# A hybrid decoder layer on one core: all projections first, attention, inverses and recurrence one or more stages behind

## The chip, the cores and the metric

One core of a Trainium2 chip runs one program; the time is device microseconds of one execution. The engines are TensorE (PE, matmuls, with its weight loads as PEld), VectorE (DVE), ScalarE (ACT), GpSimd (POOL) and SyncE (SP, which here issues nearly all DMAs). Each runs its own instructions in order and waits on semaphores for the others.

## The reference

Cut to what is computed: 2,048 new positions and 8 sequences of 8 decoded ones go through one layer of width 1024.

```
h = rmsnorm(x, norm_attn);  p = h @ w_in                  # 512 q, 128 k, 128 v, 1792 rwkv, 2048 gates
o_attn = sliding-window attention (window 128, sinks), 8 q heads on 2 kv heads
o_rwkv = RWKV-7 on the 1792: token shift, lora decay w and rate a, then per position
         S = S * w + (S a) b^T + v k^T ;  y = S r           # 8 heads, S is 64 x 64
         group norm, bonus, gate
merged = sigmoid(g0) * (o_attn @ w_branch_attn) + sigmoid(g1) * (o_rwkv @ w_branch_rwkv)
x = x + merged @ w_out
u = rmsnorm(x, norm_ffn) @ w_ffn_in                        # 2 x 2816
x = x + (gelu(causal conv of width 3 over u0) * u1) @ w_ffn_out
y = rmsnorm(x, norm_final)                                 # and the new caches and states
```

## The kernel before

**Tiling.** The 2,112 columns (positions, then decoded tokens) are cut into three blocks of 704, and a block into halves of 384 and 320. Values lie transposed, features on partitions. Weights and activations are float32, each split into a high part and a rest (`split`, `unit`), and a product is three matmuls: high by high, high by rest, rest by high (`mm3`). A unit is one load of 128 x 1024 weights; ACT casts its high part (L335), and POOL or, for every third unit, DVE computes the rest (L341). A unit meets one block in 48 matmuls, 24 for each half. These dense matmuls write the tile `psd` (three PSUM banks); everything else on PE uses `psr` (three banks) and `psc` (two).

**Stages of a block.** `inputs`: 36 units of `w_in`, of which 14 feed the recurrence (`proj_rwkv`, with `prep` and `keynorm` making per-chunk operands, written to DRAM), 6 attention, and 16 the gates. Then `attn_prompt` (pieces of 128 positions by two groups of heads), `inverse` (per half, triangular inverses of 64 x 64 by elimination on DVE), `recur` (`chain`: 11 chunks of 64 positions, each with three handovers from PE to DVE or ACT and back, then `groupnorm`), `gather` (loads the branch outputs and splits them into the operand `os`), `merge` (8 units of `w_br` and 8 of `w_out`), and `ffn` (66 units).

**What sets the order.** The code emits dense work in sequence. Background work consists of generators in queues (`push`); before each k-step `mm3` calls `tick`, and `step` advances a generator by one piece when a model of the engines' clocks says that its operands will be there (`account`, `open`). `drain` advances queues without any dense work until they are empty. A scheduler then fixes each engine's order. Before, `inputs(0)` runs with the load of the next `h` beside it; `rest(0)` (attention and inverses together, then the recurrence) is queued behind it and runs beside `inputs(1)`. Four gate units of block 1 are held back; `early_merge` queues the gather of block 0, runs them, drains, and merges. The FFN of block 0 has `rest(1)` and `next_h(2)` beside it; then `inputs(2)`, the merge of block 1, its FFN with `rest(2)` and the gather of block 2, and the merge and FFN of block 2.

**Names in the steps.** `h` is the split, normed input of a block (two buffers in turn); `normed` (L431, L345, L346) makes one of its eight columns. `cvu`, `cm`, `car`, `ckb`, `cq` are the operands of a chunk, loaded one chunk ahead (L1103 and around), `cx` the solution's copy (L1121), `S` the state (L1164, L1165). `ol` are the branch outputs in `gather` (L1277), two buffers; `gt` the gate tiles (two). LAG (L30) puts the last tiles of `w_out` in the order (6,0), (7,0), (6,1), (7,1). In an inverse L1057 and L1063 are transposes of 32 x 32 blocks.

Of the kernel before, what the change touches and what calls it, by code (L numbers as in the profile page):

```python
# [17 lines left out]
P = 128  # L18
# [30 lines left out]
for _name, _w in (("ident", 128), ("maskp", 128), ("sel", 2), ("selm", 2), ("ones", 1), ("cj", 128),  # L49
                  ("blk", 128), ("bm", 8), ("m65", 390), ("att", 256), ("masks", 128), ("m65s", 332)):  # L50
    CST[_name] = (_n, _w)
    _n += _w
# [50 lines left out]
class Kernel:  # L103
    def __init__(self, tc, i, o, es):
# [8 lines left out]
        self.kp_ = pool("keep", 2)  # L113
# [5 lines left out]
        self.anchor, self.inside = {}, False  # L119
# [40 lines left out]
    def setup(self):  # L160
# [3 lines left out]
        for name in ("cj", "blk"):  # L164
            self.cr[name] = cp.tile([P, CST[name][1]], F32R, name=f"{name}r")
            nc.gpsimd.tensor_copy(self.cr[name], self.cst(name))
# [71 lines left out]

    def account(self):
# [4 lines left out]
        for k in range(self.seen, m):  # L244
# [5 lines left out]
            if engine in ("DVE", "Activation"):  # L250
                if self.inside:
                    if engine in self.anchor:
                        self.tc.add_manual_dep(ins, self.anchor[engine], mybir.DependencyInfo(
                            mybir.DependencyClass.NoSync, mybir.DependencyReason.DATA), reason="after the dense work before it")
                elif any(hasattr(a, "bass_ap") and a.bass_ap.tensor.name.startswith("psd") for a in ins.ins):
                    self.anchor[engine] = ins.name
            if engine == "PE":
                t["PE"] += c
# [16 lines left out]
    def tick(self):  # L275

        self.account()
        for q in self.streams.values():
            self.step(q)
# [5 lines left out]
    def step(self, q):  # L285
        t = self.clock
        if not q or q[0][1] > t["PE"] or self.open() > t["PE"]:
            return
        self.account()
        entry = q[0]  # L290
        self.inside = True
# [14 lines left out]
        entry[1] = max(entry[1], at + entry[3])  # L306

# [143 lines left out]
    def start(self, hp, xp):  # L451
# [4 lines left out]
        self.ct = self.cp.tile([P, CST["m65"][0]], F32, name="ct")  # L456
# [12 lines left out]
        nc.sync.dma_start(self.ct, self.i["cst"][:, :CST["m65"][0]])  # L469
# [41 lines left out]
    def load_h(self, b, hp):  # L511

        h = self.bigtile(hp, "h")
        self.push("n", self.load_steps(b, h))
        return h
# [97 lines left out]
    def attn_prompt(self, b, ap):  # L613
        nc = self.nc
        npr = T if b < 2 else T - TS
# [51 lines left out]
        items = [(t0, g) for t0 in range(0, npr, 128) for g in range(2)]  # L667
        fs = {0: front(0)}
        yield 4.0
        fs[0] = halves(fs[0])  # L670
        fr = front(128)
        yield 0.2
        sm = {0: (yield from head(fs[0], 0))}
# [295 lines left out]
    def mtile(self, b, pp, name):  # L969


        if b == 1 and name == "kt":
            return self.tp.tile([P, 2, 384], F32, tag="xv", name="kt", bufs=2)[:].rearrange("p a c -> p (a c)")[:, :512].rearrange("p (c j) -> p c j", j=128)
        return pp.tile([P, 4, 128], F32, tag="m", name=name, bufs=2 if b == 1 else 4)

    def headsum(self, sq, sel, least, eps, k):

        nc = self.nc
        nt = 3 * sq.shape[1]
# [743 lines left out]
```

## Time and profile before

| what | value |
|---|---|
| runs shown | 3412.99 us median of three (3409.52 to 3416.1) |
| profiled execution | 3416.34 us, span 3414.6 us |
| mean granted PE clock | 0.978 |
| busy, share of the span | PE 96%, PEld 93%, DVE 57%, ACT 36%, POOL 30% |
| matmuls, and weight loads | 24,072 each |
| DMA | 416.02 MB, 122 GB/s on average |

A row of the profile gives line, engine, operation, written tile<-read tiles with shapes, and a count; then busy time, mean ns of one, and the engine's idle time before them with who ended it. A row by stage gives its start and end, its length, busy time with count for each engine (or for one tile), the granted clock, the DMA share and GB/s. A timeline row gives start and length, and in brackets the wait before it and what ended it. A float32 matmul that is not split counts twice in the trace and once in the order of instructions.

### The profile page before, as it was taken

The page shows a single profiled execution, that of the slowest core. Times are in us where ns is not written, and L with a number is a line of the kernel's source. Part 1 is how long each engine was busy: PE and PEld are TensorE (multiplying, and loading weights), DVE is VectorE, ACT ScalarE, POOL GpSimd, SP SyncE. Part 2 cuts the span into 40 slices and gives each one's busy share as a digit, 9 for nine tenths or more (in the row PEclk, how much of TensorE's full clock was granted, in tenths as well). Part 3 has the DMA queues.
Part 4 walks back from the last instruction along what each step waited for, and adds up shares of the span by engine and source line. Part 5 has one row for each costly group of instructions (what it writes and reads, how often), then busy time and mean ns, then how long its engine had stood idle before and what let it go on. Part 6 is the DMA issues. An engine that isn't in the chain of part 4 may idle for free.

```text
span 3414.6 us, 60708 instructions
## 1 busy us (share of the span) xinstructions
PE 3294.5 (96%) x24072; PEld 3164.2 (93%) x24072; DVE 1950.5 (57%) x4088; ACT 1239.6 (36%) x2286; POOL 1007.7 (30%) x870
## 2 busy tenths in 40 slices
PE   8999999986899999999999999999999999999998
PEld 7999999885898999999999999999999999999998
DVE  7566776613457764656565245865454654455455
ACT  4234534331236642323333334652222323222223
POOL 3334334210332211223433244222212254222223
PEclk9999999997999999999999999999999999999999
DMA  4456445464423334423644643334431472222222
GB/s 132 139 169 186 129 135 143 134 191 130 150 77 90 94 113 138 149 82 98 210 132 132 202 145 93 91 89 136 123 123 46 128 248 76 74 68 69 68 69 74
DMA packets 341836, 416.02 MB, mean 122 GB/s; under 512 B 110897, under 2 KB 269489, under 8 KB 341297
## 3 DMA queue, kind: packets, MB, share of 16 engines
q1 hardware_dynamic: 337392, 406.39, 39.1%
q10 hardware_dynamic: 4160, 5.77, 0.5%
q8 instruction: 189, 3.10, 0.4%
q14 instruction: 95, 0.77, 0.1%
HBM read 314.63 MB, written 98.41 MB: 121 GB/s over the span
## 4 chain that ended last, share of the span: by engine, by line
PE 72%; DVE 3%; DMA 2%; ACT 2%; issue 1%; POOL 1%; SPq 0%; POOLq 0%; DVEq 0%; ACTq 0%
PE psd L354 62%; PE psr L955 1%; PE psr L706 1%; DMA cvu<-vvd 1%; PE psc L1161 1%; PE psc L1159 1%; PE psc L982 1%; PE psc L1126 1%; PE psc L1156 1%; PE psr L658 1%; PE psr L693 1%; PE psc L1118 0%; PE psc L1255 0%; DMA gt<-gd 0%; PE psc L1153 0%
## 5 line engine op out<-in xcount | busy, mean ns | idle before, releaser
L354 PE MATMUL psd<-o,wp 128*128 128x320 f32 (+1 forms) x7488 | 1271.9, 327 | 40.4 <-ACT o L345 14.5
L354 PEld LDWEIGHTS psd<-o,wp 128*128 128x128 f32 x7488 | 1215.0, 190 | 59.1 <-ACT o L345 16.4
L341 POOL TENSOR_TENSOR wp<-wr,wp 128x512 fp32r<-128x512 f32 x472 | 653.7, 1406 | 1609.4 <-ACT wp L335 1439.1
L354 PE MATMUL psd<-h,wp 128*128 128x384 f32 (+1 forms) x6336 | 1096.2, 327 | 14.4 <-ACT wp L335 9.8
L354 PEld LDWEIGHTS psd<-h,wp 128*128 128x128 f32 x6336 | 1020.5, 189 | 29.3 <-ACT wp L335 10.3
L335 ACT CAST wp<-wr 128x1024 fp32r<-128x1024 f32 x354 | 370.9, 1048 | 624.4 <-PE psd L354 578.9
L354 PE MATMUL psd<-ff,wp 128*128 128x384 f32 (+1 forms) x3168 | 536.5, 325 | 0.5 <-DVE x L1409 0.4
L354 PEld LDWEIGHTS psd<-ff,wp 128*128 128x128 f32 x3168 | 509.1, 188 | 8.3 <-issue 3.2
L1409 DVE TENSOR_TENSOR x<-x,psd 128x384 f32<-128x384 f32 (+1 forms) x288 | 147.9, 518 | 206.1 <-PE psd L354 205.1
L1380 DVE TENSOR_TENSOR gb<-psd,rb 128x64 f32<-128x64 f32 (+2 forms) x154 | 70.4, 469 | 214.9 <-PE psd L354 198.7
L1383 DVE SCALAR_TENSOR_TENSOR cc<-gb,pt,cc 128x704 f32<-128x704 f32 (+1 forms) x132 | 170.1, 1288 | 37.3 <-ACT cc L1381 36.5
L341 DVE TENSOR_TENSOR wp<-wr,wp 128x1024 fp32r<-128x1024 f32 x118 | 147.1, 1247 | 69.1 <-ACT wp L335 66.4
L1381 ACT ACTIVATE cc<-gb,pt 128x64 f32<-128x64 f32 (+2 forms) x154 | 95.8, 636 | 178.4 <-DVE gb L1380 175.1
L346 DVE TENSOR_TENSOR ff<-cc,ff 128x384 fp32r<-128x384 f32 (+1 forms) x132 | 92.0, 698 | 40.9 <-ACT ff L345 40.3
L1392 ACT ACTIVATE cc<-cc 128x704 f32<-128x704 f32 x66 | 52.3, 793 | 150.1 <-DVE cc L1386 71.6
L395 POOL TENSOR_TENSOR acc<-acc,sq 128x320 f32<-128x320 f32 (+1 forms) x81 | 78.9, 975 | 76.5 <-ACT sq L394 74.0
L1313 DVE SCALAR_TENSOR_TENSOR m<-gt,psd 128x384 f32<-128x384 f32 (+1 forms) x96 | 49.2, 518 | 74.8 <-PE psd L354 55.9
L1373 DVE TENSOR_TENSOR up<-psd,rb 128x384 f32<-128x384 f32 (+1 forms) x132 | 68.5, 519 | 40.1 <-PE psd L354 40.0
L1316 POOL TENSOR_TENSOR m<-m 128x384 f32<-128x384 f32 (+1 forms) x48 | 47.6, 992 | 143.7 <-DVE m L1313 134.7
L345 ACT CAST ff<-cc 128x384 fp32r<-128x384 f32 (+1 forms) x132 | 63.8, 485 | 59.3 <-DVE cc L1395 57.8
L1270 ACT ACTIVATE g<-psd,der 128x384 f32<-128x384 f32 x64 | 35.4, 553 | 130.3 <-PE psd L354 85.3
L1395 DVE TENSOR_TENSOR cc<-cc,up 128x384 f32<-128x384 f32 (+1 forms) x132 | 71.2, 541 | 20.0 <-ACT cc L1392 16.3
(258 smaller groups left out, 3331.3 us busy)
## 6 DMA issues: line engine op xcount, KB each, us to landing
wr<-in_w_fi SPq DMA_DIRECT2D x132, 512.0 KB, 3.5
wr<-in_w_in SPq DMA_DIRECT2D x108, 512.0 KB, 3.8
wr<-in_w_fo SPq DMA_DIRECT2D x66, 512.0 KB, 3.5
cm<-md SPq DMA_DIRECT2D x33, 512.0 KB, 5.0
gt<-gd SPq DMA_DIRECT2D x48, 352.0 KB, 3.5
md<-m SPq DMA_DIRECT2D x48, 256.0 KB, 2.7
wr<-in_w_br SPq DMA_DIRECT2D x24, 512.0 KB, 4.2
wr<-in_w_out SPq DMA_DIRECT2D x24, 512.0 KB, 3.5
```

What stands on the lines that cost most here:

```text
L335: nc.scalar.copy(w[:, 0], raw)
L341: eng.tensor_tensor(w[:, 1, sl], raw[:, sl], w[:, 0, sl].bitcast(F32), op=ALU.subtract)
L345: self.nc.scalar.copy(hi, src)
L346: (eng or self.nc.vector).tensor_tensor(lo, src, hi.bitcast(F32), op=ALU.subtract)
L354: nc.tensor.matmul(ps[:, :n], w[:, a, wk * 128:(wk + 1) * 128], act[:, k0 + k, b, c0:c0 + n], start=(start and k == 0 and j == 0), stop=(s ...
L395: eng.tensor_tensor(acc, acc, sq[:, :n], op=ALU.add)
L1373: nc.vector.tensor_tensor(up[:, c0:c0 + n], ps[:, :n], rb[:, c0:c0 + n], op=ALU.mult)
L1380: nc.vector.tensor_tensor(dst, view(ps, 0), view(rb, c0), op=ALU.mult)
L1381: nc.scalar.activation(view(c, c0), dst, ACT.Identity, bias=self.par("cb", f), scale=cw[2])
L1383: nc.vector.scalar_tensor_tensor(c[:, :npr], gb[:, u:u + npr], cw[u], c[:, :npr], op0=ALU.mult, op1=ALU.add)
L1395: nc.vector.tensor_tensor(cv, cv, up[:, c0:c0 + n], op=ALU.mult)
L1409: nc.vector.tensor_tensor(xv, xv, ps[:, :n], op=ALU.add)
```

## The change

- `run`: the inputs of blocks 0, 1, 2 come one after the other. Beside them run attention of block 0, then the inverses of block 0, then the recurrence of block 0 and attention of the first 256 positions of block 1. Beside the merge and FFN of block 0: the rest of block 1's attention, all of block 2's, the inverses and recurrence of block 1, and the gather of block 1. Beside the merge and FFN of block 1: inverses and recurrence of block 2, and its gather.
- `load_x`, `switch`: the next block's `x` is loaded into a tile of its own and its norm computed during a block's inputs; the last two gate units write the new `h` over the old, a half at a time.
- `gather` uses four buffers; gate tiles are loaded two ahead (`gate_tiles`) ahead of the merge; `x` is loaded at the third unit of `w_br`.
- `inverse`: one transpose of 128 partitions and two ACT copies take the place of four transposes of 32.
- `w_out` tiles in plain order, also the first FFN units; streams are served in the order of when each last ran; PE instructions of one piece keep their order; some tiles change pools.

```diff
-LAG = tuple((j, h) for j in range(6) for h in range(2)) + ((6, 0), (7, 0), (6, 1), (7, 1))
...
+    def load_x(self, b, xp):
+        self.xn, self.xr = xp.tile([P, KT, T], F32, name="xn"), []
...
+    def switch(self, b, ws, js):
+        for hf, (c0, n) in enumerate(HALF):
+            for w, j in zip(ws, js):
+                ps = self.dbank()
+                self.mm3(ps, w, self.h, c0, n)
+                self.gate(b, j, hf, ps if b else self.timed(ps, hf))
+            for k in range(KT):
+                self.normed(self.h, k, c0, n, self.xn[:, k, c0:c0 + n], self.xr[hf])
...
+        nc.vector.transpose(q[:, :, 32:].rearrange("p b t -> p t b"), qb)
         for r in range(2):
             o = 64 - r * 64
-            for u in range(2):
-                rows = slice(o + 32 * u, o + 32 * u + 32)
-                yield
-                nc.vector.transpose(q[rows, :, 32 * u:32 * u + 32].rearrange("p b t -> p t b"), qb[rows])
+            nc.scalar.copy(q[o:o + 32, :ns, :32], q[o:o + 32, :ns, 32:])
...
-            t = pool.tile([P, T], F32, tag="ol", name="ol", bufs=2)
+            t = pool.tile([P, T], F32, tag="ol", name="ol", bufs=4)
...
-        for j, hf in LAG:
+        for j, hf in ((j, hf) for j in range(8) for hf in range(2)):
...
-                for r, hf in (((0, 0), (1, 0), (0, 1), (1, 1)) if f == 0 else ((0, 0), (0, 1), (1, 0), (1, 1))):
+                for r, hf in ((0, 0), (0, 1), (1, 0), (1, 1)):
...
+            if p:
+                self.drain("r")
...
+        with self.pool("early") as ep:
+            self.inputs(0, ep, [self.attention(0)])
+            self.inputs(1, ep, [self.inverses(0)])
+            self.inputs(2, ep, [self.chunks(0), self.attention(1, 0, 256)], HOLD)
...
+        self.push("c", self.gathered(0, os_))
...
+            gts = self.gate_tiles(0, gp)
+            self.gates(2, range(16 - HOLD, 16))
+            self.drain("c")
+            hs.close()
+            self.push("c", self.attention(1, 256), self.attention(2), self.inverses(1), self.chunks(1))
...
+                self.branches(0, os_, ms, gts, x)
+                xs = self.merge(0, x, ms, xp, op)
+        for b in (1, 2):
...
+            self.push("c", ahead())
+            self.ffn_stage(b - 1, *xs)
+            self.drain("c")
...
+                self.branches(b, os_, ms, gts, x)
+                if b == 1:
+                    self.push("c", self.inverses(2), self.chunks(2))
+                xs = self.merge(b, x, ms, xp, op)
```

Three places in PE's order. Both kernels have the same number of dense (16,992) and small (4,120) matmuls there. The first is the end of block 0's recurrence. Before, on PE, after the last projection of block 1: the last chunk (L1126 to L1161), the group norm, and the first branch matmuls (`psd<-o`):

```order
L1153 MATMUL psc<-car,S_210 64x64 x8
L1126 MATMUL psc<-cx,cq 64x64 x8
L1161 MATMUL psc<-cm,cvu 64x64
L1159 MATMUL psc<-cvu,ckb 64x64 x8
L1161 MATMUL psc<-cm,cvu 64x64 x7
L367 MATMUL psc<-parts,cjr 128x320 x8
L982 MATMUL psc<-ct,gsq 128x2 x12
L1016 MATMUL psc<-ct,grb 128x128 x3
L1255 MATMUL psc<-gs,gup 128x320
```

These are the last of 576 small matmuls in a row. Now, on PE, a chunk of the same recurrence in the middle of block 2's projections (lines moved: L1126 is L1162, L1159 is L1195, L1161 is L1197; `rbk` belongs to block 2's preparation):

```order
L1189 MATMUL psc<-car,S_214 64x64 x8
L366 MATMUL psd<-h,wp 128x384 x3
L366 MATMUL psd<-h,wp 128x320 x15
L1162 MATMUL psc<-cx,cq 64x64 x8
L366 MATMUL psd<-h,wp 128x320 x9
L366 MATMUL psd<-h,wp 128x384 x6
L1053 MATMUL psr<-ct,rbk 128x128 x3
L366 MATMUL psd<-h,wp 128x384 x8
L1195 MATMUL psc<-cvu,ckb 64x64 x8
L1197 MATMUL psc<-cm,cvu 64x64 x8
L366 MATMUL psd<-h,wp 128x384 x10
L366 MATMUL psd<-h,wp 128x320 x15
```

Each handover of the chunk now has 15 to 25 dense matmuls behind it.

The second is the start of the first merge. Now, on PE, from the last projections of block 2 (`psd<-h`) over the end of block 1's early attention (`psr<-ct,s`, `psr<-pT,v`) to the first branch matmuls:

```order
L366 MATMUL psd<-h,wp 128x320 x5
L992 MATMUL psr<-ar,kb 128x128
L730 MATMUL psr<-ct,s 128x128 x8
L743 MATMUL psr<-pT,v 64x256 x2
L730 MATMUL psr<-ct,s 128x128 x4
L743 MATMUL psr<-pT,v 64x256 x2
L730 MATMUL psr<-ct,s 128x128 x4
L743 MATMUL psr<-pT,v 64x256 x4
L366 MATMUL psd<-o,wp 128x384 x13
L366 MATMUL psd<-o,wp 128x320 x13
```

And on SP at that place, the DMAs of the gather (`ol`) among the attention's write (`od`) and the next attention piece's loads (`q`, `k`, `v`):

```order
L748 DMA od_227<-ot 128x2x128
L667 DMA k<-kd_221 64x256
L671 DMA v<-vd_224 128x128
L1316 DMA ol<-od_226 128x704 x4
L671 DMA v<-vd_224 128x128
L665 DMA q<-qd_218 64x4x128 x3
L1316 DMA ol<-rd_0_282 128x704
L1316 DMA ol<-rd_1_283 128x704
```

The gather stands behind 24 small matmuls of attention where it stood behind the recurrence; its first four loads go out together, and the loads of `x`, which stood between its first and second pair, come after its last.

The third is the switch from block 0 to block 1. Before, PE goes from unit to unit in halves of 24:

```order
L354 MATMUL psd<-h,wp 128x384 x24
L354 MATMUL psd<-h,wp 128x320 x24
L354 MATMUL psd<-h,wp 128x384 x24
L354 MATMUL psd<-h,wp 128x320 x24
L354 MATMUL psd<-h,wp 128x384 x24
```

Now, on PE, the second halves of the last two gate units (the 48), then block 1's first two units:

```order
L366 MATMUL psd<-h,wp 128x320 x48
L366 MATMUL psd<-h,wp 128x384 x2
L366 MATMUL psd<-h,wp 128x320
L366 MATMUL psd<-h,wp 128x384 x12
L366 MATMUL psd<-h,wp 128x320 x2
L366 MATMUL psd<-h,wp 128x384 x12
L366 MATMUL psd<-h,wp 128x320
L366 MATMUL psd<-h,wp 128x384 x21
L366 MATMUL psd<-h,wp 128x320 x9
L366 MATMUL psd<-h,wp 128x384
L366 MATMUL psd<-h,wp 128x320 x35
```

The first halves of both units (48) come nearly whole before the second halves, whose `h` is written last.

More of the change, by code (lines that the diff above doesn't have):

```diff
@@ L237, in cost, with after @@
         return 0.1 + (0.0012 if len(full) > 1 else 0.0009) * n
+    def after(self, ins, name):
+        self.tc.add_manual_dep(ins, name, mybir.DependencyInfo(mybir.DependencyClass.NoSync, mybir.DependencyReason.DATA),
+                               reason="order on the engine")
     def account(self):
@@ L252, in account @@
                     if engine in self.anchor:
-                        self.tc.add_manual_dep(ins, self.anchor[engine], mybir.DependencyInfo(
-                            mybir.DependencyClass.NoSync, mybir.DependencyReason.DATA), reason="after the dense work before it")
+                        self.after(ins, self.anchor[engine])
                 elif any(hasattr(a, "bass_ap") and a.bass_ap.tensor.name.startswith("psd") for a in ins.ins):
@@ L257, in account @@
             if engine == "PE":
+                if self.inside:
+                    if self.before:
+                        self.after(ins, self.before)
+                    self.before = ins.name
                 t["PE"] += c
@@ L1319, in merge, with load_x1 @@
                 nc.vector.scalar_tensor_tensor(lo, m[0][:, :n], 0.5, hi.bitcast(F32), op0=ALU.mult, op1=ALU.subtract)
+        next(gts, None)
+    def load_x1(self, b, x):
+        with self.tc.issue_after(self.load):
+            for k in range(0, KT, 2):
+                self.nc.sync.dma_start(x[:, k:k + 2], self.i["xT"][:, k:k + 2, b * T:(b + 1) * T])
+    def merge(self, b, x, ms, xp, op):
+        nc = self.nc
         h2 = self.bigtile(op, "o")
@@ L1509, in rwkv_prep, with inputs @@
             between(p)
-    def inputs(self, b, ahead=None, hold=0):
+    def inputs(self, b, ep, background, hold=2):
         nc = self.nc
@@ L1549, in inputs, with attention, inverses, chunks @@
                         nc.sync.dma_start(self.o[new][:, :, :120], self.i[old][:, :, 8:])
[L1550 to L1553 removed]
+    def attention(self, b, t0=0, t1=T):
         with self.pool("att", side="right") as ap:
[L1556 removed]
+            yield from self.attn_prompt(b, ap, t0, t1)
             if b == NB - 1:
[L1558 to L1559 removed]
+                yield from self.attn_sample(ap)
+    def inverses(self, b):
+        with self.pool("inv", side="right") as ip:
+            for hf in range(2):
+                yield from self.together((1.4, [self.inverse(b, hf, ip)]))
+    def chunks(self, b):
         with self.pool("chain", 2, side="right") as kp:
             yield from self.recur(b, kp)
[L1563 to L1566 removed]
     def recur(self, b, kp):
```

250 lines of the change are left out of this document (134 added, 116 removed).

## The prediction

> **What bounds the kernel now.** First the page: who is busy, and where in the span.
>
> ```profile
> PE 3294.5 (96%) x24072; PEld 3164.2 (93%) x24072; DVE 1950.5 (57%) x4088; ACT 1239.6 (36%) x2286; POOL 1007.7 (30%) x870
> PE   8999999986899999999999999999999999999998
> PEclk9999999997999999999999999999999999999999
> ```
>
> TensorE (PE) is busy 96% of the span. The tenth slice (768 to 854 us) is the only one at 6, and the granted clock drops to 7 there too. So the next view is busy time by stage, first of the dense matmuls alone (tile `psd`, count in brackets). I cut the stages where the work changes; 340 to 720 us is the second block's projections with the first block's attention and inverses between them.
>
> ```profile
> 340.00:720.00 380.00, 307.96 (x1725) 0.99 0.46 133
> 720.00:873.00 153.00, 25.12 (x109) 0.75 0.57 177
> 1000.00:1250.00 250.00, 202.58 (x1162) 0.97 0.31 87
> 1250.00:1620.00 370.00, 324.84 (x1879) 1.00 0.40 124
> 2900.00:3380.00 480.00, 480.00 (x2985) 1.00 0.22 69
> ```
>
> And all engines, in the order PE, PE's weight loads, DVE (VectorE), ACT (ScalarE), POOL (GpSimd):
>
> ```profile
> 340.00:720.00 380.00, 371.59 (x2719) 350.36 (x2718) 245.15 (x569) 172.67 (x395) 123.38 (x105) 0.99 0.46 133
> 720.00:873.00 153.00, 105.03 (x1269) 84.72 (x1267) 47.27 (x118) 28.76 (x68) 10.21 (x11) 0.75 0.57 177
> 1000.00:1250.00 250.00, 236.04 (x1697) 218.81 (x1698) 194.46 (x449) 136.13 (x284) 62.83 (x43) 0.97 0.31 87
> 1250.00:1620.00 370.00, 369.38 (x3175) 353.93 (x3174) 205.69 (x387) 119.11 (x196) 91.96 (x71) 1.00 0.40 124
> 1620.00:1920.00 300.00, 296.15 (x1902) 285.50 (x1901) 169.19 (x386) 105.84 (x192) 108.98 (x115) 1.00 0.53 159
> ```
>
> The last row of the dense matmuls gives the yardstick: with nothing beside it a dense matmul takes 480.00/2985 = 0.161 us. The edit leaves these as they are; only what is not dense can move. From 720 to 873 us 109 dense matmuls are worth 17.5 us, so 135.5 of the 153 us go to 1,160 small matmuls (the first block's recurrence, nearly all of it), to waits, and to a clock at 0.75. Other blocks' recurrences run between dense matmuls: from 1250 to 1620 us 1,296 small ones cost 370 - 1879 x 0.161 = 67.5 us, 0.052 us each, with PE idle 0.6 us.
>
> **The change, part by part.** *The uncovered recurrence.* In the new PE order it stands among the third block's projections, with at most 32 small matmuls in a row before that stage ends. 1,160 at 0.052 are 61 us in place of 135.5: **-75 us**. Its lower end is a span with little but chain matmuls beside the dense ones:
>
> ```profile
> 1300.00:1350.00 50.00, 39.37 (x225) 1.00 0.49 152
> ```
>
> ```profile
> 1300.00:1350.00 50.00, 50.00 (x561) 46.28 (x561) 21.26 (x39) 10.87 (x17) 11.19 (x8) 1.00 0.49 152
> ```
>
> There (50 - 225 x 0.161)/336 = 0.041 us, which would make it -88; at the (380 - 1725 x 0.161)/994 = 0.103 us of the 340 to 720 stage, where preparation shares VectorE, only -16, the upper end. I take 0.052, from a row that holds a whole recurrence with its group norm. The stage it moves into has room: in 1620 to 1920 VectorE (DVE) is busy 56%, ScalarE (ACT) 35%, GpSimd (POOL) 36%. Its chunk loads go on SP's queue, two buffers deep:
>
> ```profile
> 722.81 7.93 DMA cvu<-vvd
> ```
>
> ```profile
> PE psc L1161 <- ACT cvu L1129: 6.4, 11, 1.4
> ```
>
> A late chunk load took 7.9 us. The new order puts some 55 dense matmuls (9 us) and the small ones between chunks, so a prefetched chunk is just covered. Of the three handovers of a chunk the longest-waiting one cost 0.6 us on average (6.4 us in 11).
>
> *What is late next: the gather.* Before the first merge the branch outputs are still loaded and split with no dense work. In 720 to 873 us that is the last 30 us:
>
> ```profile
> 844.46 0.87 SPq L1277 DMA_DIRECT2D ol<-od  x2
> 845.39 2.02 SPq L1299 DMA_DIRECT2D x<-in_xT  x4
> 849.38 1.26 SPq L1277 DMA_DIRECT2D ol<-od  x2
> 858.47 6.42 SPq L1277 DMA_DIRECT2D ol<-rd  x4
> ```
>
> Its last splits on ACT, the landing time of its second four loads, and the group of exponentials that a piece of attention ends with:
>
> ```profile
> 867.85 0.87 ACT L345 CAST o<-ol 128x384 fp32r<-128x384 f32 x2 [1.14 <-DMA ol<-rd]
> ```
>
> ```profile
> ol<-rd SPq DMA_DIRECT2D x4, 352.0 KB, 3.1
> ```
>
> ```profile
> L601 ACT ACTIVATE s<-s,nm 128x256 f32<-128x256 f32 (+2 forms) x136 | 65.8, 485 | 41.5 <-DVE nm L596 41.4
> ```
>
> It took 24 us, because only two buffers were there and 2.8 MB of `x` went in between. The first term counts all of it as gone, so what comes back is charged here. In the new order the gather still stands behind the held gates, after the last two items of a piece of attention: four exponentials at 0.49 us, as many scalings of the same tiles, and transposes, copies and a write, about 6 us. Then four loads at once (3 to 6 us to land), four more as buffers come free, and 16 splits of 0.48 us on ACT: about 11 us. Off 17 us I take 48 first branch matmuls (7.7 us) and 2 us of attention on PE. **+8 us**; ends +4 (some tail hidden) and +20 (as slow as now).
>
> *The inverses.* Four transposes of 32 rows become one of 128:
>
> ```profile
> L1063 DVE STREAM_TRANSPOSE qinv<-qb 32x1024 f32<-32x1024 f32 x24 | 48.3, 2011 | 0.5
> L1057 DVE STREAM_TRANSPOSE t<-qb 128x1024 f32<-128x1024 f32 x6 | 13.3, 2210 | 0.0
> ```
>
> ```profile
> 637.23 1.22 PE L955 MATMUL psr<-ar,kb 64*128 64x128 f32 x4 [2.07 <-DVE pT L700]
> ```
>
> That is 4 x 2.01 - 2.21 = 5.8 us of DVE in each of six inverses, for two ACT copies. DVE is not the bound, so only the PE waits behind these transposes count; PE idles 8.4 us in the whole 340 to 720 stage and 2.07 us of it is the row above. **-5 us** (0 to -10).
>
> *The two early FFN stages.* Attention and inverses ran together at their start:
>
> ```profile
> 1028.66 2.18 PE L354 MATMUL psd<-o,wp 128*128 128x384 f32 x6 [6.82 <-ACT wp L335]
> ```
>
> ```profile
> L601 ACT ACT_TABLE_LOAD x12 | 15.4, 1283 | 4.6 <-DVE nm L596 4.4
> L1392 ACT ACT_TABLE_LOAD x16 | 20.5, 1283 | 30.8 <-DVE cc L1383 29.6 <-DVE rs L604 1.1
> ```
>
> ```profile
> 2100.00:2250.00 150.00, 143.22 (x1075) 133.69 (x1073) 113.43 (x283) 94.59 (x202) 43.58 (x30) 0.97 0.36 98
> ```
>
> PE idled 14.0 us from 1000 to 1250 and 6.8 from 2100 to 2250, once 6.8 us behind a weight cast that ACT had not reached between exponentials, table loads and GELU. Now attention sits among projections and in the first merge, and only its end meets an FFN: **-12** (0 to -21). Beside projections it costs something: the 340 to 720 stage, with preparation, attention and inverses together, idled 8.4 us in all. **+5** (0 to +15). Dropping the staggered last tiles of `w_out` (LAG) moves both rows of the FFN's norm behind less dense work; PE waited 1.2 us there, and I leave it at 0 (0 to +5 for each block; it is inside the upper end).
>
> *Gate tiles.* The third merge waits for one (`m` is the product with the gate, late for its tile):
>
> ```profile
> 2762.08 3.30 PE L354 MATMUL psd<-o,wp 128*128 128x320 f32 x11 [6.19 <-DVE m L1313]
> ```
>
> Loading two ahead during the FFN removes it: **-6** (0 to -6).
>
> *The switch.* `h` of the next block is now written over that of this one. Per half, eight columns each need a DVE product, an ACT cast, and a rest on DVE or POOL, through two shared temporaries:
>
> ```profile
> L431 DVE SCALAR_TENSOR_TENSOR h<-xv,pt,psc 128x384 f32<-128x384 f32 (+1 forms) x32 | 17.8, 574 | 3.9 <-DMA xv<-in_xT 2.6 <-PE psc L1016 1.2
> L345 ACT CAST h<-h 128x384 fp32r<-128x384 f32 (+1 forms) x32 | 15.2, 482 | 16.7 <-DVE h L431 16.6
> L346 POOL TENSOR_TENSOR h<-h 128x384 fp32r<-128x384 f32 (+1 forms) x16 | 18.2, 1136 | 32.4 <-ACT h L345 32.3
> ```
>
> A pair of columns takes 0.57 + 0.48 + 1.14 = 2.2 us, a half 8.8, both 17 us. Beside them PE has 48 matmuls of the second half (7 us) and, by the order, the first half of the next two units (48, 8.4 us): 2 us uncovered, 3 with handovers. Twice: **+6**; with no cover +34, with perfect cover 0.
>
> **The sum:** -75 + 8 - 5 - 12 + 5 - 6 + 6 = -79 us. The profiled execution took 3416.3 us (span 3414.6), so 3337; the median shown is 3413.0, 3.3 lower: **3334 us**.
>
> **Rivals.** (1) *Crowded projections.* Recurrence and preparation fight over DVE and ACT, and a small matmul costs 0.08 to 0.10 us: 1,160 x 0.04 = 46 us come back, **3380**. For it: 0.103 in the 340 to 720 stage. Against: that stage holds dearer kinds of small matmuls, and idles little.
>
> (2) *Slower.* Each of 11 chunks has three handovers PE to DVE or ACT and back, and PE runs in order, so dense matmuls stand behind a late one. If preparation's operations (0.5 to 0.9 us each) queue ahead of each copy, the wait is paid 33 times. It turns the sign from 79/33 = 2.4 us each; at 3 us it is +99 - 79, **3433**. Against: 0.6 us, the worst average in the quiet stretch, and 0.6 us of idle in the 370 us with a recurrence beside the FFN.
>
> (3) *A shared port.* Two rows of the same microsecond:
>
> ```profile
> 1006.79 1.26 DVE L379 TENSOR_TENSOR nwtd<-nwtd,rmsm 128x3 f32<-128x3 f32 x1
> ```
>
> ```profile
> 1006.61 2.73 POOL L341 TENSOR_TENSOR wp<-wr,wp 128x512 fp32r<-128x512 f32 x2 [8.04 <-ACT wp L335]
> ```
>
> And one group over the whole span and from 720 to 873 us:
>
> ```profile
> L1165 DVE TENSOR_TENSOR S<-S,pc 128x256 f32<-128x256 f32 x32 | 16.1, 504 | 1.0
> ```
>
> ```profile
> L1165 DVE TENSOR_TENSOR S<-S,pc 128x256 f32<-128x256 f32 x11 | 4.7, 425 | 0.4
> ```
>
> A three-column product took 1.26 us while POOL split weights. The state update is 425 ns where POOL is nearly idle and 504 ns over all. POOL is busy 36% in the projections and 25% beside the FFN, so moved work meets it more; if each of 11 updates waits out a 1.4 us POOL operation, 15 us come back: **3349**. The Trainium skill (GPSIMD Engine Reference, Specifications) speaks against the move in this way: GpSimd shares its SBUF interfaces with VectorE, in contention with VectorE instructions that have two SBUF inputs. By that rule the three-column product and the update are hit and PSUM reads are not; the trace agrees in kind, with 79 ns on average; 11 times that is 0.9 us, and the forecast leaves it out.
>
> (4) *It does not do it:* the recurrence is late and the merge drains it as now, **3413**. The PE order shows no such stretch, so it would need a wait the order cannot show.
>
> (5) *Better:* chain matmuls at 0.041, no idle at the FFN starts, **3300**.
>
> **How the numbers follow.** Forecast 0.59 (3310 to 3362), shared port 0.05, crowded 0.15, better 0.10, no effect 0.03, slower 0.08. A measurement here can tell about 0.2%, 7 us. Faster 0.59 + 0.05 + 0.15 + 0.10 = 0.89, same 0.03, slower 0.08. The lower ends together are -88 + 4 - 10 - 21 + 0 - 6 + 0 = -121. The range runs from that, 3292, to 3392 (crowded with a slow gather), leaving out some 0.04 below and 0.14 above.
>
> **What would show it.** Right: no slice below 8 after the first; the third block's projections with some 1,100 more small matmuls at about 0.05 us and PE idle under 10 us; one PE gap under 12 us before the first branch matmul, ended by `ol` casts; gaps of 2 to 4 us at the two switches; no `gt` wait. Wrong: PE waits on `cx`, `cvu` or a `cvu` load adding up to over 40 us in the projections; a switch over 10 us; the gather as long as now; or DVE over 85% busy in any stage.

## The result and the profile after

The changed kernel takes **3325.57 us** (median of four runs, 3323.05 to 3327.79), the kernel before 3412.91 us on the same chip (3409.52 to 3416.1): a ratio of 0.9744, 95% interval 0.9727 to 0.9761. That is 87 us less, where 79 were forecast (3334 us). The time lies in the forecast's own range and on its side.

The page of the changed kernel, as shown of before: busy times, then PE and its clock in 40 slices.

```profile
PE 3250.5 (98%) x24072; PEld 3131.5 (94%) x24072; DVE 1948.6 (59%) x4058; ACT 1213.4 (36%) x2274; POOL 1010.1 (30%) x878
PE   8999998999999899999999999999999999999998
PEclk9999999999999899999999999999999999999999
```

The slice at 6 is gone; its place is taken by an 8 in the fourteenth slice (1081 to 1164 us), where the clock shows 8 too. The span is 3326.0 us, so PE idles 75.5 us, against 3414.6 - 3294.5 = 120.1 before. The other 44 us of the 88.6 between the two spans are time in which PE was shown busy: where small matmuls follow each other slowly, much of the time between them is recorded as busy (105.0 of the 153 us from 720 to 873 before, with only 17.5 us of dense work).

By stage, the dense matmuls alone (tile `psd`). 390 to 740 us are block 1's projections with the inverses of block 0, 740 to 1130 block 2's with the recurrence of block 0, 1130 to 1165 the passage to the first merge.

```profile
390.00:740.00 350.00, 298.17 (x1723) 0.99 0.45 135
740.00:1130.00 390.00, 306.32 (x1728) 1.00 0.54 167
1130.00:1165.00 35.00, 15.29 (x63) 0.76 0.78 241
```

And all engines (PE, weight loads, DVE, ACT, POOL), with the start of the first FFN, 1320 to 1570 us, as a last row:

```profile
390.00:740.00 350.00, 336.04 (x2463) 323.89 (x2463) 219.04 (x453) 130.69 (x239) 114.05 (x112) 0.99 0.45 135
740.00:1130.00 390.00, 387.00 (x3304) 364.18 (x3302) 203.94 (x489) 145.11 (x295) 121.51 (x121) 1.00 0.54 167
1130.00:1165.00 35.00, 21.65 (x114) 17.37 (x114) 12.62 (x27) 16.08 (x38) 5.33 (x4) 0.76 0.78 241
1320.00:1570.00 250.00, 247.57 (x1915) 236.29 (x1915) 175.90 (x384) 100.74 (x187) 59.01 (x47) 0.99 0.28 79
```

The same projections of block 2 in the kernel before had no recurrence beside them. First the dense matmuls, then all engines:

```profile
1625.00:1960.00 335.00, 298.49 (x1734) 1.00 0.55 168
```

```profile
1625.00:1960.00 335.00, 331.15 (x2122) 320.50 (x2121) 173.01 (x392) 117.58 (x213) 111.77 (x116) 1.00 0.55 168
```

Beyond its dense work at 0.161 us each the stage took 335 - 1734 x 0.161 = 55.8 us before and 390 - 1728 x 0.161 = 111.8 us now, with 388 and 1,576 small matmuls: 1,188 more (1,160 of them are as many as the uncovered stretch held before) for 56.0 us, **0.047 us each**, PE idle for 3.0 us. No wait on `cx`, `cvu` or a chunk's load is among PE's waits after (first the total, then how often, then the longest):

```profile
PE psd L366 <- ACT o L357: 10.8, 2, 7.9
...
PE psr L1053 <- DVE rbk L1031: 5.8, 1, 5.8
PE psd L366 <- DVE m L1364: 5.6, 4, 3.7
PE psd L366 <- DVE wp L353: 3.8, 2, 3.6
...
PE psd L366 <- DVE xs L832: 1.7, 2, 0.9
```

The largest waits left between the program's first norm and its last are the gather (`o`), one of the key norms (`rbk`), one product with a gate at the second merge (`m`, 3.7 us) and one weight rest at the second FFN (`wp`, 3.6 us); the two switches cost 0.9 us each (`xs`). The passage to the first merge, in order of time, SP being the queue of loads:

```profile
1142.14 0.37 ACT L747 COPY ot<-psr 128x256 f32<-128x256 f32 x1 [2.10 <-DMA od<-ot]
1142.57 0.53 SPq L748 DMA_DIRECT2D od<-ot  x1
...
1144.35 1.80 SPq L1316 DMA_DIRECT2D ol<-od  x4
...
1148.62 4.48 PE L366 MATMUL psd<-o,wp 128*128 128x384 f32 x12 [7.88 <-ACT o L357]
...
1149.92 1.02 SPq L1316 DMA_DIRECT2D ol<-rd  x2
...
1155.49 0.87 ACT L357 CAST o<-ol 128x384 fp32r<-128x384 f32 x2 [3.88 <-DMA ol<-rd]
...
1156.05 6.14 PE L366 MATMUL psd<-o,wp 128*128 128x384 f32 x24 [2.95 <-ACT o L357]
```

Its 35 us held 63 dense matmuls (10.1 us) and 51 small ones (2.7 us at 0.052), so some **22 us** were lost. By the same count the gather lost 23 before (844.4 to 873 us, with 36 dense matmuls). The first four loads go out at 1144.4 us, after the last write of attention (`od`), which waits for a copy into `ot`, which waits 2.1 us for the write before it out of the same tile. From issue to landing the eight loads took (least, median, longest)

```profile
DMA to landing us min/median/max: 3.6/5.3/7.0
```

The second four, from `rd`, go out between 1149.9 and 1152.7 us, each within half a microsecond of the split that frees its buffer, and take 5.5 to 7.0 us to land.

### The profile page after: what moved, and what is told of

The parts are those of the page before. It is cut to its first block, busy times and chain, and to the rows that moved or that the text cites. A ratio compares the mean times of both kernels' runs of the same rounds, so it can differ in the third digit from the quotient of the medians.

```text
span 3326.0 us, 60594 instructions
## 1 busy us (share of the span) xinstructions
PE 3250.5 (98%) x24072; PEld 3131.5 (94%) x24072; DVE 1948.6 (59%) x4058; ACT 1213.4 (36%) x2274; POOL 1010.1 (30%) x878
## 4 chain that ended last, share of the span: by engine, by line
PE 71%; DVE 3%; DMA 1%; issue 1%; ACT 0%; POOL 0%; SPq 0%; POOLq 0%; DVEq 0%; ACTq 0%
PE psd L366 62%; PE psr L694 1%; PE psr L743 1%; PE psc L1162 1%; PE psc L1195 1%; PE psc L1192 1%; DVE qt L1088 1%; DVE qb L1090 1%; PE psr L730 1%; DMA xd<-x 0%; PE psr L992 0%; PE psc L1019 0%; PE psc L1197 0%; PE psc L1291 0%; PE psc L1189 0%
## 5 line engine op out<-in xcount | busy, mean ns | idle before, releaser
L366 PE MATMUL psd<-o,wp 128*128 128x320 f32 (+1 forms) x8640 | 1453.6, 326 | 21.1 <-ACT o L357 10.8
L366 PEld LDWEIGHTS psd<-o,wp 128*128 128x128 f32 x8640 | 1400.9, 189 | 32.6 <-ACT o L357 11.8
L366 PE MATMUL psd<-h,wp 128*128 128x320 f32 (+1 forms) x5184 | 918.1, 330 | 15.2 <-ACT wp L347 7.4
L366 PEld LDWEIGHTS psd<-h,wp 128*128 128x128 f32 x5184 | 838.4, 190 | 30.8 <-ACT wp L347 7.4
L366 PE MATMUL psd<-ff,wp 128*128 128x384 f32 (+1 forms) x3168 | 526.7, 325 | 0.0
L353 DVE TENSOR_TENSOR wp<-wr,wp 128x1024 fp32r<-128x1024 f32 x119 | 148.1, 1244 | 88.5 <-ACT wp L347 84.7
L407 POOL TENSOR_TENSOR acc<-acc,sq 128x320 f32<-128x320 f32 (+1 forms) x93 | 95.0, 1023 | 115.5 <-ACT sq L406 97.4
L1090 DVE TENSOR_TENSOR qb<-qb,qt 128x31 f32<-128x31 f32 (+15 forms) x186 | 88.9, 478 | 4.1
L1088 DVE TENSOR_TENSOR qt<-nb,qb 128x31 f32<-128x31 f32 (+15 forms) x186 | 84.6, 455 | 3.2
```

What stands on the lines that cost most here:

```text
L353: eng.tensor_tensor(w[:, 1, sl], raw[:, sl], w[:, 0, sl].bitcast(F32), op=ALU.subtract)
L366: nc.tensor.matmul(ps[:, :n], w[:, a, wk * 128:(wk + 1) * 128], act[:, k0 + k, b, c0:c0 + n], start=(start and k == 0 and j == 0), stop=(s ...
L407: eng.tensor_tensor(acc, acc, sq[:, :n], op=ALU.add)
L1088: nc.vector.tensor_tensor(tv, nb[:, s + 1:, s:s + 1].to_broadcast([P, k, s + 1]), qb[:, s:s + 1, :s + 1].to_broadcast([P, k, s + 1]), op=A ...
L1090: nc.vector.tensor_tensor(qb[:, s + 1:, :s + 1], qb[:, s + 1:, :s + 1], tv, op=ALU.add)
```

## The experiments

Each ran beside runs of the kernel before on its chip; times are medians of four runs and more, ratios are to the kernel before with 95% intervals. "The changed kernel" stands at 3325.57 us and 0.9744 (0.9727 to 0.9761). Edits are to the changed kernel except in one case.

**1. The recurrence uncovered again.**

```diff
-            self.inputs(2, ep, [self.chunks(0), self.attention(1, 0, 256)], HOLD)
+            self.inputs(2, ep, [self.attention(1, 0, 256)], HOLD)
+        self.push("c", self.chunks(0))
+        self.drain("c")
```

> The changed kernel with one thing undone: the recurrence of block 0 is queued only after block 2's inputs and drained there, so 456 small matmuls stand in a row again. Coverage theory (the gain is mostly the recurrence put between dense matmuls): bare it took about 124 us from 720 to 844 us in the kernel before with some 9 us of dense work in it, covered it costs 45 to 60, so +40 to +60 us on 3326: 3366 to 3386, with PE's clock under 0.9 in that stretch. Rival (the gain is mostly from the other edits, transposes, gather, gate tiles, FFN starts): at most +15, 3341.

Measured: 3379.91 us, ratio 0.9912 (0.9897 to 0.9926), so 54 us slower than the changed kernel. The dense matmuls in the last stretch before the merge, and the wait of the recurrence:

```profile
1100.00:1195.00 95.00, 3.06 (x7) 0.72 0.48 141
```

```profile
PE psc L1195 <- DVE cvu L1166: 14.9, 8, 8.0
```

Seven dense matmuls in 95 us, the granted clock at 0.72, and PE waits of 14.9 us for a handover of the chunks that the changed kernel does not have at all. From 1100 to 1187 us 712 small matmuls take 87 us, 0.12 us each. The cover is worth about 54 of the 87 us. The gather stands uncovered in both and loses 19 us here (1187 to 1215 us, 60 dense matmuls) where the changed kernel loses 22. At the 5,200th dense matmul, counted from the start and standing in the first merge, the two kernels are 44 us apart, at the 6,800th 53: the last 9 us come in that merge and its FFN and were not followed.

**2. The gather covered: one piece of early attention fewer.**

```diff
-            self.inputs(2, ep, [self.chunks(0), self.attention(1, 0, 256)], HOLD)
+            self.inputs(2, ep, [self.chunks(0), self.attention(1, 0, 128)], HOLD)
...
-            self.push("c", self.attention(1, 256), self.attention(2), self.inverses(1), self.chunks(1))
+            self.push("c", self.attention(1, 128), self.attention(2), self.inverses(1), self.chunks(1))
```

> The changed kernel with only the first 128 instead of 256 positions of block 1's attention beside block 2's inputs, so that the gather of block 0 falls beside the four held gate units. Theory that the start of the first merge is still uncovered: from the last projection to steady branch matmuls the changed kernel takes 31 us for 48 dense matmuls (7.7 us) and about 2.6 us of small ones, some 20 us lost; most of it goes: -14 to -20 us, 3306 to 3312, with no PE wait for an ol cast over 1 us. Rival (the gather's casts and loads cost the same beside the gates, and the attention moved behind it costs as much in the merge): -5 to +3.

Measured: 3329.71 us, 0.9766 (0.9751 to 0.9781): not faster, so the expectation's theory failed and its rival held. The start of the first FFN in this kernel:

```profile
1300.00:1550.00 250.00, 238.42 (x1692) 223.40 (x1691) 162.34 (x388) 109.42 (x219) 57.37 (x45) 0.96 0.27 76
```

PE idles 11.6 us here, where the changed kernel idles 2.4 in its first 250 us of FFN and the kernel before 14.0. More attention was pushed from the first merge into the FFN, and what the gather gained was lost there: by the same dense matmul this kernel is 19 us ahead of the changed one at the 5,200th, 20 at the 6,000th and 1 at the 6,400th. So the wait at the gather and the collision of attention with the FFN are two ends of one queue.

**3. The four transposes put back.**

```diff
-        nc.vector.transpose(q[:, :, 32:].rearrange("p b t -> p t b"), qb)
         for r in range(2):
             o = 64 - r * 64
-            nc.scalar.copy(q[o:o + 32, :ns, :32], q[o:o + 32, :ns, 32:])
+            for u in range(2):
+                rows = slice(o + 32 * u, o + 32 * u + 32)
+                yield
+                nc.vector.transpose(q[rows, :, 32 * u:32 * u + 32].rearrange("p b t -> p t b"), qb[rows])
```

> The changed kernel with the inverse's four transposes of 32 rows restored, 5.8 us more of VectorE in each of six inverses, in one run of 8 us. By the forecast's term +5 us (3331), 0 to +10, with PE waits behind the transposes. Rival (VectorE is not the bound and the steps are timed by the model): within 2 us of 3326 although VectorE is 35 us busier.

Measured: 3341.11 us, 0.9802 (0.9787 to 0.9816), 15.5 us slower than the changed kernel. Two of PE's waits in it:

```profile
PE psr L1053 <- DVE rbk L1031: 9.4, 1, 9.4
...
PE psd L366 <- DVE wp L353: 7.2, 3, 3.9
```

They grow by 3.6 and 3.4 us. Of the 10.4 us between the two profiled executions 8 come in block 1's projections, beside the inverses of block 0: these take 359 us in place of 351, and PE idles 19.7 us there in place of 14.0. The edit also changes how often an inverse gives way to other work, so the longer transposes and the other places in the order are not told apart.

**4. The single transpose alone, on the kernel before** (the reverse edit).

> The kernel before with this one part of the change alone: one transpose of 128 partitions and two copies on ACT in place of four transposes of 32, in all six inverses. Undoing it in the changed kernel cost 0.6%, about 20 us, where the prediction had 5 (0 to 10). Theory: the size depends on what stands beside the inverses; in the kernel before the waits behind these transposes are about 2 to 7 us, so -3 to -10 us, 3403 to 3410 us. Rival: each transpose holds PE up wherever it stands, 35 us of VectorE in all; then -15 to -30 us, 3383 to 3398 us.

Measured: 3403.52 us against 3413.77, 0.9973 (0.9964 to 0.9983): 10 us faster, at the upper edge of what the theory expected. So this part is worth 10 us alone and 15 in its new place, where the forecast had 5 (0 to 10).

**5. No early attention.**

```diff
-            self.inputs(2, ep, [self.chunks(0), self.attention(1, 0, 256)], HOLD)
+            self.inputs(2, ep, [self.chunks(0)], HOLD)
...
-            self.push("c", self.attention(1, 256), self.attention(2), self.inverses(1), self.chunks(1))
+            self.push("c", self.attention(1), self.attention(2), self.inverses(1), self.chunks(1))
```

> As the run with 128 positions, but with no attention of block 1 at all beside block 2's inputs; all of it comes with the first merge. Theory that only the gather's cover matters: the same as with 128 positions within 5 us. Rival (attention beside projections is dear, 0.10 us a small matmul, and cheaper in the merge): 5 to 10 us faster than with 128 positions. Second rival (the merge and FFN of block 0 are then too full): slower by 5 us or more, with waits of PE on ACT weight casts at the FFN's start.

Measured: 3320.81 us, 0.9739 (0.9723 to 0.9756), within the uncertainty of the changed kernel. PE has no wait on `o` any more, since the recurrence ends before the projections do, and the gather with it; but the first FFN, which begins 33 us earlier in this kernel, starts like this:

```profile
1287.00:1537.00 250.00, 241.18 (x1725) 223.79 (x1724) 163.94 (x397) 123.51 (x262) 60.00 (x46) 0.97 0.29 82
```

PE idles 8.8 us against 2.4: again attention beside the FFN. By the 6,000th dense matmul this kernel is 36 us ahead, at the 6,800th 10.

**6. Attention by block**: as 5, and the attention of block 2 moved on to the second merge and FFN.

```diff
-            self.push("c", self.attention(1), self.attention(2), self.inverses(1), self.chunks(1))
+            self.push("c", self.attention(1), self.inverses(1), self.chunks(1))
...
-                    self.push("c", self.inverses(2), self.chunks(2))
+                    self.push("c", self.attention(2), self.inverses(2), self.chunks(2))
```

> The changed kernel with all attention of block 1 ahead of the first merge's matmuls (none beside the last projections) and the attention of block 2 moved from the first merge and FFN to the second. Without the early attention alone the time stayed (3320.8 us, ratio 0.9739): the gap at the gather went, and 30 us came back in the first FFN. Theory: that FFN was too full, and with the attention of block 2 in the second merge and FFN its excess over dense work falls from 135 to about 100 us while the second merge and FFN gain 35 to 45: 3310 to 3325 us. Rival: the second FFN then has the collision in turn (attention beside GELU, or the gather of block 2 not done at its end), over 3330 us.

Measured: 3314.57 us, 0.9714 (0.9699 to 0.9728): 11 us faster than the changed kernel; the two intervals just touch. The first merge, the start of the first FFN (33 us earlier here too), and the start of the second FFN:

```profile
1125.00:1295.00 170.00, 167.05 (x1079) 151.99 (x1077) 111.31 (x267) 100.67 (x256) 73.12 (x62) 1.00 0.47 138
1287.00:1537.00 250.00, 244.31 (x2246) 235.76 (x2245) 158.27 (x330) 78.39 (x123) 58.46 (x47) 0.99 0.37 112
2035.00:2280.00 245.00, 243.52 (x1883) 234.97 (x1882) 168.12 (x357) 91.29 (x159) 57.24 (x48) 0.98 0.31 88
```

PE idles 3.0, 5.7 and 1.5 us, and has no wait on `o` any more. When each of the first two merges and FFNs has one block's attention, the gap at the gather goes, and only some 3 us of it come back at the first FFN (5.7 against 2.4).

**7. Attention queued only ahead of the first FFN.**

```diff
-            self.push("c", self.attention(1, 256), self.attention(2), self.inverses(1), self.chunks(1))
             with self.pool("ms") as mp:
...
+        self.push("c", self.attention(1, 256), self.attention(2), self.inverses(1), self.chunks(1))
         for b in (1, 2):
```

> The changed kernel with the rest of the attention of blocks 1 and 2, the inverses and the recurrence of block 1 queued only ahead of the first FFN, not ahead of the first merge. This tests the term of the early FFN stages (forecast -12, about -16 read from the changed profile). Theory: attention meets the FFN's GELUs and table loads again, PE waits of 5 to 7 us at the start of that FFN come back, +8 to +20 us, 3333 to 3346 us. Rival: the merge gives back what the FFN pays, the same within 0.2%. Second way to be slower: the stream no longer fits into that FFN and what is left of the gather of block 1 is drained without dense work; then over 3350 us with a PE gap ahead of the second merge's branch matmuls.

Measured: 3363.78 us, 0.9858 (0.9844 to 0.9873), 38 us slower. PE's waits for the gather's casts, and two rows at the second merge:

```profile
PE psd L366 <- ACT o L357: 33.8, 4, 16.8
```

```profile
1949.18 0.81 PE L1291 MATMUL psc<-gs,gup 128*128 128x320 f32 x2 [2.85 <-DVE y L1292]
...
1965.40 1.60 PE L366 MATMUL psd<-o,wp 128*128 128x384 f32 x3 [15.42 <-ACT o L357]
```

This is the second way of the expectation: the work no longer fits beside one FFN, the group norm and the gather of block 1 come out behind its end, and PE stands 15.4 us. The gather of block 0 is also later (16.8 us in place of 7.9): loads of `x` and then of `v` stand ahead of it on SP's queue, and its first loads go out at 1153.7 us in place of 1144.4. The run does not tell what the FFN's starts alone are worth; runs 2 and 5 do.

**8. The staggered tiles and the old order of the first FFN units put back.**

```diff
-        for j, hf in ((j, hf) for j in range(8) for hf in range(2)):
+        for j, hf in tuple((j, h) for j in range(6) for h in range(2)) + ((6, 0), (7, 0), (6, 1), (7, 1)):
...
-                for r, hf in ((0, 0), (0, 1), (1, 0), (1, 1)):
+                for r, hf in (((0, 0), (1, 0), (0, 1), (1, 1)) if f == 0 else ((0, 0), (0, 1), (1, 0), (1, 1))):
```

> The changed kernel with the staggered last tiles of w_out and the old order of the first FFN units put back. The prediction left this edit at 0 (0 to +5 a block): the norm of the FFN then has more dense work in front of it, and the waits on it (about 1 and 3.6 us at the starts of the FFNs in the changed kernel) go or stay. Theory: the same time within 0.2%, 3319 to 3333 us. Rival: the plain order is what costs the waits at the FFN starts, then 5 to 10 us faster, 3316 to 3320 us. Other rival: the plain order is a part of the gain, then over 3333 us.

Measured: 3325.03 us, 0.9746 (0.9730 to 0.9762). This part is worth nothing, as forecast.

**9. Two buffers in the gathers.**

```diff
-            t = pool.tile([P, T], F32, tag="ol", name="ol", bufs=4)
+            t = pool.tile([P, T], F32, tag="ol", name="ol", bufs=2)
...
-        ts = deque(load(k) for k in range(4 - 1))
+        ts = deque(load(k) for k in range(2 - 1))
```

> The changed kernel with two buffers instead of four in the gathers. In the changed kernel the gap ahead of the first branch matmuls, from the last projection at 1133.2 us to steady matmuls at 1156.1, lost about 20 us where the prediction had 8. Theory: the loads themselves bind this gap (two at once, each about 3 us to land), so two buffers lose 4 to 10 us more there: 3329 to 3336 us. Rival: the tail of the attention ahead of the gather binds it, and the number of buffers changes nothing: 3320 to 3329 us.

Measured: 3336.91 us, 0.9780 (0.9767 to 0.9793), 11 us slower, just over what the theory gave. The loads on SP's queue:

```profile
1147.57 1.02 SPq L1316 DMA_DIRECT2D ol<-od  x2
...
1149.21 2.13 SPq L1376 DMA_DIRECT2D x<-in_xT  x4
...
1153.08 13.08 SPq L1316 DMA_DIRECT2D ol<-rd  x4
```

The four loads of `rd` wait for buffers, each in turn, and stand behind 2.8 MB of `x`, as in the kernel before. Four buffers are worth 11 us to the change.

**10. The first gather loaded from POOL's queue.**

```diff
-            self.nc.sync.dma_start(t, self.od[b][:, k] if k < 4 else self.rd[b][k - 4])
+            (self.nc.gpsimd if b == 0 else self.nc.sync).dma_start(t, self.od[b][:, k] if k < 4 else self.rd[b][k - 4])
```

> The changed kernel with the gather of block 0 loaded from POOL's queue in place of SP's, where the first loads stand behind the last write of attention (`od`) and the loads of the next piece (`q`, `k`, `v`). Theory: the loads were late because of the queue they stand in; on POOL, idle from 1138 to 1145 us, they go out up to 5 us sooner and the gap shrinks by 3 to 6 us: 3318 to 3323 us. Rival: the buffers come free only when the tail of the attention has ended, so the loads go out no sooner and the time stays, 3322 to 3330 us.

Measured: 3334.47 us, 0.9771 (0.9757 to 0.9784), 9 us slower: worse than either side expected. On POOL:

```profile
1144.25 2.35 POOL L358 TENSOR_TENSOR q<-q,q 128x1024 fp32r<-128x1024 f32 x1 [6.76 <-ACT q L357]
1146.53 2.30 POOL L1316 DMA_DIRECT2D ol<-od  x4
1153.88 0.54 POOL L1316 DMA_DIRECT2D ol<-rd  x1 [5.04 <-DVE o L358]
```

POOL runs in order too, and there the loads stand behind the split of the next piece's `q`, which waits for its cast; the gather's go out at 1146.5 us instead of 1144.4. They also land later: SP's queue, free of the gather, sends the first loads of `x` at 1144.7 us, and the gather's first four take 5.5 to 7.8 us in place of 3.6 to 5.0. Whether the `x` loads or the other queue lengthen them, and whether the buffers would have been free earlier, stays open.

**11. Gate tiles not loaded ahead.**

```diff
-        for j in range(2):
-            load(j)
         for j in range(8):
+            load(j)
             yield gts.popleft()
-            if j < 6:
-                load(j + 2)
```

> The changed kernel with each gate tile loaded only when its unit of w_br is taken up, not two ahead. The prediction gave this part -6 (0 to -6). Theory: without the two tiles ahead the first products with a gate are late in each merge, a PE wait on `m` of 3 to 6 us in one or more of the three merges: +3 to +12 us, 3329 to 3337 us. Rival: the two buffers cover the load whoever asks first, and the time stays within 0.2%.

Measured: 3324.96 us, 0.9743 (0.9730 to 0.9756); PE's waits on `m` are

```profile
PE psd L366 <- DVE m L1361: 4.7, 4, 3.7
```

against 5.6 us in the changed kernel. Asking two tiles ahead is worth nothing, as the rival had it.

**12. The rests of all weights on VectorE.**

```diff
-        eng = nc.gpsimd if self.nw % 3 else nc.vector
+        eng = nc.vector
```

> The changed kernel with the rests of all weight units computed on VectorE, where two units in three were GpSimd's. GpSimd loses 648 us of work and is busy about 11% in place of 30%; VectorE gains about 270 us and is busy about 67%. This tests the shared port, rival 3 of the prediction. Theory: the port stretches small operations of VectorE (128 x 12 and 128 x 3: mean 190 to 270 ns, single ones 0.9 to 1.2 us beside GpSimd) but few of them are waited for: their mean falls to 160 to 190 ns, the 5.8 us wait on `rbk` shrinks to under 4, and the time moves by -10 to +10 us, 3316 to 3336 us. Rival: the port costs 15 us and more, then under 3312 us. Other rival: VectorE, 270 us busier, makes PE wait on operands: over 3340 us.

Measured: **3296.29 us**, 0.9657 (0.9644 to 0.9671), 29 us faster than the changed kernel: the first rival of the expectation. The page of this kernel, and its stage of block 1's projections:

```profile
PE 3247.3 (98%) x24072; PEld 3130.4 (95%) x24072; DVE 2002.0 (61%) x4294; ACT 1217.2 (37%) x2276; POOL 367.6 (11%) x406
```

```profile
390.00:740.00 350.00, 348.26 (x2562) 337.02 (x2561) 230.66 (x502) 140.03 (x253) 56.53 (x67) 1.00 0.48 144
```

PE idles 1.7 us in that stage in place of 14.0. Groups of VectorE by shape, of the changed kernel and then of this one (total, then mean ns):

```profile
L353 DVE TENSOR_TENSOR wp<-wr,wp 128x1024 fp32r<-128x1024 f32 x119 | 148.1, 1244 | 88.5 <-ACT wp L347 84.7 <-POOL parts L358 1.5 <-issue 1.0
...
L358 DVE TENSOR_TENSOR ff<-cc,ff 128x320 fp32r<-128x320 f32 x66 | 55.7, 843 | 16.5 <-ACT ff L357 16.3
```

```profile
L353 DVE TENSOR_TENSOR wp<-wr,wp 128x1024 fp32r<-128x1024 f32 x354 | 442.8, 1251 | 171.6 <-ACT wp L347 164.9 <-DMA cvu<-vvd 2.9
...
L358 DVE TENSOR_TENSOR ff<-cc,ff 128x320 fp32r<-128x320 f32 x66 | 32.0, 485 | 0.3 <-ACT ff L357 0.3
```

The rests add 442.8 - 148.1 = 295 us to VectorE, yet its busy time rises by only 2002.0 - 1948.6 = 53 us: its other work became 241 us shorter without GpSimd's 643 us beside it. Three changes run together here: the contention, the shorter rest itself (1.25 us for a unit on VectorE, two times 1.4 on GpSimd), and PE's order, since the program places its small matmuls by a model of the engines' clocks. Over the whole kernel half of the small matmuls stand at least 21 dense ones away from their old place. In block 1's projections the order is nearly the same (528 of 740 small matmuls within three dense ones of it), and these projections take 334 us in place of 351. PE's waits there on VectorE (`rbk` 5.8 us, `kt` 2.0, `vt` 1.8, `kb` 1.3, `kk` 1.1) are gone, and on a rest it had waited only 0.8 us. So some 16 of the 29 us belong to the contention; the rest is not settled. Runs 6 and 12 together were not tried.

## Why the forecast was right, step by step

**The recurrence.** The -75 counted the whole stretch as gone, 24 us of gather in it; without them it was -75 + 24 = -51. Run 1 gives -54 (with 9 us from later stages in it), and the stage shows why: 0.047 us for a small matmul, against the 0.052 taken from the recurrence beside the FFN and the 0.103 that the crowded rival feared. Mechanism and size held. The slower rival needed 2.4 us at every handover; PE has no such wait in the changed kernel.

**The gather** was the step that failed in size. +8 were charged (ends +4 and +20), 22 came. "About 17 us" had two parts: 6 us for the tail of attention and 11 for loads and splits. The tail took 11 us, from the last projection matmul at 1133.2 us to the loads at 1144.4. About 2 us of that are the wait of its last copy for the write before it, through one `ot` tile, and another 1.2 us are loads of `k` and `v` that stand ahead of the gather's; the forecast had neither. Loads and splits took another 16, to 1160.6: the second four loads go out as buffers come free, as forecast, but take 5.5 to 7.0 us to land, where the row of before had 3.1. What lengthens them was not tested. The sign named for this, "the gather as long as now", is what the trace shows. The four buffers helped (run 9, 11 us), and the tail and the slow landings took it back.

**The inverses**: -5 (0 to -10) was too small: 10 us alone on the kernel before, 15 in the changed kernel. The step that counted only the one PE wait seen behind a transpose (2.07 us) missed what else VectorE's 35 us of relief (six times 5.8) spares: by run 3 mostly in block 1's projections (8 us), where the key norms wait for VectorE too.

**The FFN starts**: -12 forecast. PE idles 2.4 us in 1320 to 1570 where it idled 14.0, and at the second start one wait of 3.6 us is left of 6.8, so about -15. The mechanism, attention meeting the FFN, is shown from the other side by runs 2 and 5, where more of it sits there and PE idles 11.6 and 8.8 us.

**Beside the projections** (+5). Attention of block 0 now runs beside block 0's own projections: PE idles 4.4 us from 45 to 390 us there, and idled 0.0 from 45 to 340 before, with no attention beside them. The stage with the inverses idles 14.0 us where attention and inverses together idled 8.4. That makes +4 and +6, twice what was charged, within the range; the second has no term in the forecast, and run 12 takes it away.

**Gate tiles** (-6): the wait in the third merge went, and `m` fell from 9.6 to 5.6 us in all, but not through the two tiles ahead (run 11). What moved it stays open; the number was near and its reason wrong. **The switch** (+6) cost 0.87 us twice: the nearly perfect cover at the low end of its range. **LAG** (0): 0 (run 8).

The sum by these: -54, -2 for the gather (22 in place of 24), -10 to -15, -15, +4, +6, -4, +2, so -73 to -78 where 87 were measured. The +6 was read with the shorter transposes in place, and 8 us of their gain lie in the same stage, so these count twice; 9 to 22 us are not placed. The terms furthest off, gather (+14) and inverses (-5 to -10), went opposite ways: that the sum came within 8 us is in part luck.

**The shared port** was left out of the forecast at 0.9 us, with 15 us as a rival. Run 12 is 29 us faster without most of it, some 16 of them in block 1's projections, at the key norms and the preparation. The stage with the recurrence beside it gains nothing there (409 us in place of 407), so leaving the port out of the recurrence's term was right, and the forecast looked for its price in the wrong stage. The contention was in the kernel before as well (the row of `ff` had a mean of 826 ns there); what it costs that kernel was not run, nor what it took of the change's gain.

## What to carry to other kernels

A serial chain of small matmuls belongs beside the densest stage that has room on VectorE and ScalarE; its price there can be read from another stretch of the same trace where it is already covered. When a stall is removed, follow what stands in the load queue ahead of the next stage: the tail of the work that was moved there can take the stall's place. Before giving GpSimd a share of two-input work to relieve VectorE, compare VectorE's whole busy time with and without it, not the one operation.

## What the runs showed of the hardware

Single small operations of VectorE take up to seven times as long beside GpSimd. The steps of a key norm, 128 x 12 each (least, median and longest ns of 36), of the changed kernel and then of the kernel of run 12:

```profile
L390 DVE SCALAR_TENSOR_TENSOR nwtr<-nwyr x36: 158/170/1183, 53.7 to 999.4; 128x12 f32<-128x12 f32 x36
L391 DVE TENSOR_TENSOR nwtr<-nwtr,hsmr x36: 158/170/1186, 53.9 to 999.6; 128x12 f32<-128x12 f32 x36
```

```profile
L390 DVE SCALAR_TENSOR_TENSOR nwtr<-nwyr x36: 151/170/173, 58.2 to 973.3; 128x12 f32<-128x12 f32 x36
L391 DVE TENSOR_TENSOR nwtr<-nwtr,hsmr x36: 161/170/172, 58.4 to 973.5; 128x12 f32<-128x12 f32 x36
```

The median is the same; the longest falls from seven times the median to the median. (The third step of each round, L392, still reached 741 ns once.) In the changed kernel three in a row were hit while GpSimd computed rests, and the 5.8 us wait on `rbk` is behind them:

```profile
566.09 0.92 DVE L392 SCALAR_TENSOR_TENSOR nwyr<-nwtr,nwyr 128x12 f32<-128x12 f32 x1
567.04 1.18 DVE L390 SCALAR_TENSOR_TENSOR nwtr<-nwyr 128x12 f32<-128x12 f32 x1
568.26 1.19 DVE L391 TENSOR_TENSOR nwtr<-nwtr,hsmr 128x12 f32<-128x12 f32 x1
```

The Trainium skill (SBUF — State Buffer, Who interferes with whom) says that a VectorE instruction with two SBUF inputs contends with a GpSimd instruction that reads SBUF. These rows agree in kind, and run 12 gives the size for this kernel: 241 us of VectorE time for 643 us of GpSimd work. A step with one input (L387, 128 x 12, median 173 ns) is held in the same way: it took 1.00 us from 915.7 us on, while a GpSimd operation ran from 915.6 to 916.6, so two inputs are not a condition here.

Also unexpected: moving the first gather's loads to POOL's queue, idle at that place, made them go out 2 us later and land 4.0 to 5.4 us later, and the kernel 9 us slower: a queue that looks empty can be waiting, since each engine takes its instructions in order.
